# Block sums of the second MLP weights: VectorE additions replaced by accumulating transfers

## Chip, cores and metric

The kernel runs on one core of a Trainium2 chip. The metric is the device time of one execution in microseconds (us). It was 1401.65 us, the median of three runs (1401.09 to 1402.0).

## What is computed

Two layers of an encoder trunk over 512 tokens of 1024 features, all in float32. Each layer is a token mixer (a gated DeltaNet in layer 0, a gated linear attention in layer 1) followed by an MLP; both are added to a scaled residual and normalised. The change lies in the MLP, which runs once in each layer:

```python
def _sq_relu_mlp(h, w1, w2):          # h 512x1024, w1 1024x4096, w2 4096x1024
    a = jax.nn.relu(jnp.matmul(h, w1))
    return jnp.matmul(a * a, w2)

x = _layernorm(DEEPNORM_ALPHA * x + _sq_relu_mlp(x, mlp_w1[i], mlp_w2[i]), ln2_g[i], ln2_b[i])
```

## The kernel before

Every float32 matrix product runs as three TensorE products of split operands (`mm3`, L109 to L111): each operand is written as a high part (a ScalarE cast, L90) plus a low part (a VectorE subtraction, L91). `split` makes the pair. The names are `wh`/`wl` for the first weights and those of the mixers, `w2h`/`w2l` for the second MLP weights, `ah`/`al` for activations, `xth`/`xtl` for the transposed input of a stage. Weights reach SBUF by transfers that SyncE issues (L45); `wst` and `w2r` are the tiles in which they land.

`mlp` cuts the 4096 hidden features into G = 4 groups of 1024, that is eight blocks of 128 features each. A call of `feature` makes one such block: 24 matmuls of 512 columns into a bank `pj`, then ReLU and square on ScalarE into `h`. For the first three groups the second matrix product (512 tokens x 1024 hidden times 1024 hidden x 1024 outputs) is done by `second` with seven products of half size instead of eight, after Strassen and Winograd. The activations are four quarters `a11` to `a22`, the weights four blocks `b11`, `b12`, `b21`, `b22`, which the code names `blocks[i, j, q]` with (i, j) = (0, 0), (0, 1), (1, 0), (1, 1), and with q = 0, 1 for the two halves of a block's rows. One half is a tile `w2r` of 128 partitions x 1024 float32, 512 KB. Each product is 24 matmuls into two banks out of X, Y or Z. `nxt` puts one `feature` of the next group behind each product, so TensorE alternates: product, feature, product, feature. A group has 7 products and 8 features.

The products need sums of weight blocks. Before the change VectorE makes them: `sums` (L295, L296, L298) replaces b11 by b11 + b12 and b12 by b12 + b22, and writes b11 + b12 + b22 into two more tiles, blocks (2, 2); L359 then adds that to b21. Product 5 uses b11 + b12, product 7 uses b12 + b22, product 6 uses the sum of three, product 4 the sum of all four. The order is 1, 2, 6, 5, 7, 3, 4.

The rings limit how far things run ahead: three pairs `w2h`/`w2l`, two pairs `ah`/`al`, ten raw tiles `w2r`, three of `wst` and of `wh`/`wl`. The order within each engine is fixed when the program is built; an engine executes its queue in that order, and an instruction that waits holds back all that stand behind it on its engine. In the MLP of layer 0 GpSimd (POOL) also builds eight masks for layer 1 (`sel_masks`: tiles `tmp`, made by a memset and two selects at L463, L465 and L467), which VectorE turns into `mu1` to `mu128`. The last group goes through `last`, which the change does not touch. `load_ln` (L173) fetches the parameters of a normalisation by transfers that POOL issues.

Of the kernel before, what the change touches and what calls it, by code (L numbers as in the profile page):

```python
# [13 lines left out]
ALU = mybir.AluOpType  # L14
# [3 lines left out]
P = 128  # L18
# [232 lines left out]
def mlp(c, w1, w2, g, b, out=None, extra=None):  # L251
# [3 lines left out]

    tc, nc = c.tc, c.nc
    V, A, T = nc.vector, nc.scalar, nc.tensor
    G = 4  # L260
# [3 lines left out]
    with c.banks(pj=2, X=2, Y=2, Z=2), tc.tile_pool(name="mlp", bufs=2) as pool:  # L264
        par = c.load_ln(g, b, lambda i: pool.tile([P, 512], F32, name=f"ln{i}", bufs=1))
        touched = set()
        blocks = {}
        parts = {}
        RING = {"ah": ("ah", "al", 2), "w2": ("w2h", "w2l", 3), "raw": ("w2r", "w2r", 10)}

        def ring(name):
            return (pool, *RING[name])

        def act(ps, h):
            A.activation(h, ps, AF.Relu)  # L275
            A.activation(h, h, AF.Square)

        def raw():
            return pool.tile([P, 2, 512], F32, name="w2r", tag="w2r", bufs=10)

        def load(gi, i, j):
            for q in range(2):
                blocks[i, j, q] = t = raw()
                r = (gi * GF + i * HF + 2 * q) * P
                c.dma(t, w2[r:r + 2 * P, 512 * j:512 * j + 512].rearrange("(k p) n -> p k n", p=P))

        def split(i):

            i_, j_ = {1: (0, 0), 2: (1, 0), 3: (1, 1), 4: (1, 0), 5: (0, 0), 6: (2, 2), 7: (0, 1)}[i]
            parts[i] = [c.split(blocks[i_, j_, q], [P, 2, 512], pool=ring("w2")) for q in range(2)]  # L290

        def sums(q):

            b11, b12, b22 = (blocks[k + (q,)] for k in ((0, 0), (0, 1), (1, 1)))
            V.tensor_tensor(b11, b11, b12, ALU.add)  # L295
            V.tensor_tensor(b12, b12, b22, ALU.add)  # L296
            blocks[2, 2, q] = t = raw()
            V.tensor_tensor(t, b11, b22, ALU.add)  # L298

        def new_h():  # L300
            return [pool.tile([P, HF, S], F32, name="h", tag="h", bufs=3) for _ in range(2)]

        def feature(gi, f, h):
            act(c.proj_cm(w1, (gi * GF + f) * P, "pj"), h[f // HF][:, f % HF, :])

        def pair(src, where="ah"):
            return c.split(src, [P, HF, HT], pool=ring(where))

        def add(t, hf, ps, op=ALU.add):
            xs = c.xh(t)[hf]  # L310
            if (t, hf) not in touched:
                touched.add((t, hf))
                V.scalar_tensor_tensor(xs, xs, ALPHA, ps, ALU.mult, op)
            else:
                V.tensor_tensor(xs, xs, ps, op)

        def quarters(h):
            return [h[j][:, :, HT * i:HT * i + HT] for i in range(2) for j in range(2)]

        def second(gi, h, a, nxt):  # L320

            a11, a12, a21, a22 = quarters(h)

            def banks(tag):
                return [c.bank([P, 512], F32, name="p" + tag, tag=tag) for _ in range(2)]

            def product(bk, a, i, new):

                if i not in parts:
                    split(i)  # L330
                ws = parts.pop(i)
                for q, (wh, wl) in enumerate(ws):
                    for j in range(2):
                        sl = slice(j * P, (j + 1) * P)
                        for k in (2 * q, 2 * q + 1):
                            c.mm3(bk[j], a[0][:, k, sl], a[1][:, k, sl], wh[:, k % 2, :], wl[:, k % 2, :],
                                  new and k == 0, k == HF - 1, skip_group_check=True)

            X, Y = banks("X"), banks("Y")
            product(X, a, 1, True)  # L340
            load(gi, 1, 0)
            for j in range(2):
                add(j, 0, X[j])
            nxt()
            Z = banks("Z")
            product(Z, pair(a12), 2, True)
            s1 = pool.tile([P, HF, HT], F32, name="s1", tag="s1", bufs=1)
            V.tensor_tensor(s1, a22, a21, ALU.subtract)
            V.tensor_tensor(a21, a11, a21, ALU.subtract)
            V.scalar_tensor_tensor(a11, s1, -1.0, a11, ALU.mult, ALU.subtract)  # L350
            for q in range(2):
                sums(q)
            for j in range(2):
                add(j, 0, Z[j])
            nxt()
            product(X, pair(a11), 6, False)
            V.scalar_tensor_tensor(a12, a12, -1.0, a11, ALU.mult, ALU.subtract)
            for q in range(2):
                V.tensor_tensor(blocks[1, 0, q], blocks[2, 2, q], blocks[1, 0, q], ALU.add)  # L359
            for j in range(2):  # L360
                add(j, 1, X[j], ALU.subtract)
            nxt()
            product(Y, pair(s1), 5, True)
            if gi + 2 < G:
                load(gi + 1, 0, 0)
            for j in range(2):
                add(2 + j, 1, Y[j], ALU.subtract)
            nxt()
            product(X, pair(a21), 7, False)
            if gi + 2 < G:  # L370
                load(gi + 1, 0, 1)
            for j in range(2):
                add(2 + j, 0, X[j])
                add(2 + j, 1, X[j], ALU.subtract)
            nxt()
            product(Y, pair(a12), 3, False)
            if gi + 2 < G:
                load(gi + 1, 1, 1)
            for j in range(2):
                add(j, 1, Y[j], ALU.subtract)  # L380
            nxt()
            W = banks("Z")
            product(W, pair(a22), 4, True)
            for j in range(2):
                add(2 + j, 0, W[j])
            nxt()
            nxt()

        def last(gi, h):

            a = {}
            for i in range(2):
                for j in range(2):
                    a[i, j] = pair(h[j][:, :, HT * i:HT * i + HT], "raw" if i else "ah")
            ws = [c.wrows(w2, (gi * GF + 2 * (i % 4)) * P, i // 4 * 512, pool=ring("w2") if i < 3 else None if i < 6 else ring("raw"))
                  for i in range(8)]
            if out is None:
                c.new_x()
            for t in range(NT):
                sl = slice(t % 2 * P, t % 2 * P + P)  # L400
                for hf in range(2):
                    ps = c.bank([P, 512], F32, name="pl", tag="XYZ"[(2 * t + hf) % 3])
                    for k in range(GF):
                        wh, wl = ws[4 * hf + k // 2]
                        ah, al = a[t // 2, k // HF]
                        c.mm3(ps, ah[:, k % HF, sl], al[:, k % HF, sl], wh[:, k % 2, :], wl[:, k % 2, :], k == 0, k == GF - 1)
                    add(t, hf, ps)
                c.layernorm(c.xh(t), c.xh(t), par, last=out is not None)
                if out is None:
                    c.xpose(t, c.xt[t], ("pj",))  # L410
                else:
                    nc.sync.dma_start(out[t * P:(t + 1) * P, :], c.xt[t])

        h = new_h()
        specs = [(c.wcols(w1, f * P, pool=ring("ah") if f == 3 else None), "pj", ("pj", "pj", "X", "X")[f]) for f in range(4)]
        for f, ps in enumerate(c.proj_halves(specs)):
            act(ps, h[0][:, f, :])
        for f in range(4, GF):
            feature(0, f, h)
            if f == 5:  # L420
                load(0, 0, 0)
                load(0, 0, 1)
            if f == 6:
                load(0, 1, 1)
                split(1)
                a = pair(quarters(h)[0])
        if extra:
            extra(lambda: pool.tile([P, P], F32, name="tmp", tag="tmp", bufs=2))
        for gi in range(G - 1):
            more = gi + 2 < G  # L430
            nh = new_h()
            todo = iter(range(GF))

            def nxt():
                f = next(todo)
                feature(gi + 1, f, nh)
                if f == 6 and more:
                    split(1)
                    nxt.a = pair(quarters(nh)[0])

            second(gi, h, a, nxt)
            h, a = nh, nxt.a if more else None
        last(G - 1, h)
# [960 lines left out]
```

## Time and profile before

| | us |
|---|---|
| median of three runs | 1401.65 |
| the profiled execution | 1401.75 |
| its span | 1400.0 |
| TensorE (PE) busy | 1365.9 |
| VectorE (DVE) busy | 983.8 |
| ScalarE (ACT) busy | 689.5 |
| GpSimd (POOL) busy | 80.6 |

The difference between the execution and its span lies outside of what the trace shows. PE is busy nearly all of the span, at a granted clock of 0.998. The MLP of layer 0 takes the stretch from about 450 to 775 us, that of layer 1 the one from about 1060 to the end. A stretch in which PE is never idle can only become shorter if its matmuls become fewer or follow each other more closely; work on other engines shows in the time where PE has to wait for it.

### The profile page before, as it was taken

Reading aid. Unit: us, or ns where it says so; the run is one execution under the profiler, and the core shown is the slowest. Engines: PE = TensorE matmul, PEld = TensorE weight load, DVE = VectorE, ACT = ScalarE, POOL = GpSimd, SP = SyncE. Lnnn points to the kernel's source line nnn. Section 1 sums busy time; section 2 is a strip of 40 time slices with the busy share of each in tenths; the row PEclk is TensorE's granted clock in tenths of the full one; section 3 lists DMA queues with packets and bytes.
Section 4 is the critical chain, followed back from the end, with each engine's and each line's share of the span. In section 5 each row is a group of like instructions: output and inputs, shape, how many; then the busy total and the mean of one; then the engine's idle time right before and its main releaser. Section 6 shows DMA issues by size and latency. Waiting matters only on the chain.

```text
span 1400.0 us, 20133 instructions
## 1 busy us (share of the span) xinstructions
PE 1365.9 (98%) x7933; PEld 1117.6 (80%) x7933; DVE 983.8 (70%) x1589; ACT 689.5 (49%) x1320; POOL 80.6 (6%) x120
## 2 busy tenths in 40 slices
PE   7999999999999999999999999999999999999997
PEld 6777777777777888888887888888878888888886
DVE  5787787778668676758656577876766657777655
ACT  3776657665633554444543354654434444445430
POOL 5000000000003200000000100000001000000000
PEclk9999999999999999999999999999999999999999
DMA  6212111211133733332131222221216342422121
GB/s 171 76 48 60 46 46 46 61 46 46 47 106 86 230 121 94 102 122 59 45 100 40 87 87 71 61 61 61 89 48 207 107 153 61 136 75 60 46 83 52
DMA packets 146117, 117.05 MB, mean 84 GB/s; under 512 B 7631, under 2 KB 122439, under 8 KB 146023
## 3 DMA queue, kind: packets, MB, share of 16 engines
q1 hardware_dynamic: 144112, 111.49, 26.5%
q0 software_dynamic: 1344, 4.20, 1.1%
q8 instruction: 62, 1.02, 0.3%
q14 instruction: 32, 0.26, 0.1%
q10 hardware_dynamic: 567, 0.08, 0.0%
HBM read 113.66 MB, written 2.10 MB: 83 GB/s over the span
## 4 chain that ended last, share of the span: by engine, by line
PE 61%; issue 27%; ACT 6%; DVE 3%; POOL 2%; DMA 1%; DVEq 0%; POOLq 0%; SPq 0%; ACTq 0%
PE pj L110 4%; PE pj L111 4%; PE pj L109 4%; PE pjv L109 3%; PE pjv L111 3%; PE pjv L110 3%; PE scp L678 2%; PE op L1335 2%; PE pjq L110 1%; PE pjq L111 1%; PE pjq L109 1%; PE op L766 1%; PE lv L1210 1%; PE pX L109 1%; PE pX L111 1%
## 5 line engine op out<-in xcount | busy, mean ns | idle before, releaser
L91 DVE TENSOR_TENSOR wl<-wst,wh 128x1024 fp32r<-128x1024 f32 x137 | 168.5, 1231 | 165.5 <-ACT wh L90 164.8
L90 ACT CAST wh<-wst 128x1024 fp32r<-128x1024 f32 x137 | 143.9, 1051 | 267.8 <-PE pj L110 164.4
L109 PE MATMUL pj<-xth,wh 128*128 128x512 f32 (+1 forms) x544 | 201.7, 372 | 0.7 <-ACT xth L149 0.7
L110 PE MATMUL pj<-xtl,wh 128*128 128x512 f32 (+1 forms) x544 | 201.6, 371 | 0.4 <-DVE xtl L150 0.4
L111 PE MATMUL pj<-xth,wl 128*128 128x512 f32 (+1 forms) x544 | 201.7, 371 | 0.0
L91 DVE TENSOR_TENSOR w2l<-w2r,w2h 128x1024 fp32r<-128x1024 f32 x84 | 102.6, 1222 | 49.4 <-ACT w2h L90 48.9
L110 PEld LDWEIGHTS pj<-xtl,wh 128*128 128x128 f32 x544 | 102.5, 188 | 18.7 <-DVE xtl L150 0.9
L109 PEld LDWEIGHTS pj<-xth,wh 128*128 128x128 f32 x544 | 102.3, 188 | 18.3 <-ACT xth L149 0.9
L111 PEld LDWEIGHTS pj<-xth,wl 128*128 128x128 f32 x544 | 102.4, 188 | 18.1 <-DVE wl L91 0.3
L90 ACT CAST w2h<-w2r 128x1024 fp32r<-128x1024 f32 x84 | 88.3, 1051 | 55.3 <-DMA w2r<-in_mlp_w 17.5
L90 ACT CAST ah<-h 128x1024 fp32r<-128x1024 f32 x40 | 42.2, 1054 | 56.2 <-DVE h L350 21.8
L110 PE MATMUL pX<-w2l,ah 128*128 128x512 f32 x144 | 56.1, 390 | 0.0
L109 PE MATMUL pX<-w2h,ah 128*128 128x512 f32 x144 | 56.1, 390 | 0.0
L111 PE MATMUL pX<-w2h,al 128*128 128x512 f32 x144 | 56.1, 390 | 0.0
L109 PE MATMUL pjv<-wh,xth 128*128 128x512 f32 x128 | 54.9, 429 | 0.0
L91 DVE TENSOR_TENSOR al<-h,ah 128x1024 fp32r<-128x1024 f32 x40 | 48.9, 1222 | 2.8 <-ACT ah L90 1.5
L160 ACT ACTIVATE rsy<-rsv 128x1 f32<-128x1 f32 (+1 forms) x28 | 5.6, 200 | 90.8 <-DVE rsv L159 90.8
L111 PE MATMUL pjv<-wh,xtl 128*128 128x512 f32 x128 | 50.2, 392 | 0.0
L110 PE MATMUL pjv<-wl,xth 128*128 128x512 f32 x128 | 49.9, 390 | 0.0
L109 PE MATMUL pjk<-xth,wh 128*128 128x512 f32 (+1 forms) x112 | 42.1, 376 | 0.5 <-ACT wh L90 0.5
L110 PE MATMUL pjk<-xtl,wh 128*128 128x512 f32 (+1 forms) x112 | 41.6, 371 | 0.0
L275 ACT ACTIVATE h<-pj 128x512 f32<-128x512 f32 x64 | 37.8, 591 | 7.4 <-PE pj L111 7.4
(442 smaller groups left out, 3444.8 us busy)
## 6 DMA issues: line engine op xcount, KB each, us to landing
wst<-in_mlp_w SPq DMA_DIRECT2D x80, 512.0 KB, 4.0
w2r<-in_mlp_w SPq DMA_DIRECT2D x48, 512.0 KB, 3.6
wst<-in_a_w_in SPq DMA_DIRECT2D x32, 512.0 KB, 4.0
wst<-in_b_w_in SPq DMA_DIRECT2D x32, 256.0 KB, 3.0
wst<-in_a_w_out SPq DMA_DIRECT2D x8, 512.0 KB, 3.8
wst<-in_b_w_in SPq DMA_DIRECT2D x8, 512.0 KB, 3.8
wst<-in_b_w_out SPq DMA_DIRECT2D x8, 512.0 KB, 3.6
xt<-in_x SPq DMA_DIRECT2D x4, 512.0 KB, 7.3
```

What stands on the lines that cost most here:

```text
L90: nc.scalar.copy(hi, src)
L91: nc.vector.tensor_tensor(lo, src, hi.bitcast(F32), ALU.subtract)
L109: mm(ps, ah, bh, start=start, stop=False, **kw)
L110: mm(ps, ah, bl, start=False, stop=False, **kw)
L111: mm(ps, al, bh, start=False, stop=stop, **kw)
L160: nc.scalar.activation(y, v, AF.Ln)
L275: A.activation(h, ps, AF.Relu)
L678: T.matmul(ps[:, n, :], kh[:, sl], qh[:, sl], start=True, stop=True)
L766: T.matmul(ops, l, r, start=i == 0, stop=i == len(mm) - 1)
L1210: T.matmul(ps[:, u, :, :], lhs[:, u, :], cols(rhs, u, s, i), start=True, stop=True)
L1335: T.matmul(op[:, n, :], l, r, start=i == 0, stop=i == len(mm) - 1)
```

## The change

The 48 VectorE additions (eight in each of the three groups, in two layers) are removed. In their place `plus` issues, from the POOL queue, a transfer from one SBUF tile to another that adds its source to its destination in place. There are eight of 512 KB each in a group: after the split for product 1, b11 += b12 and b12 += b22; after the split for product 5, b11 += b22 (now the sum of three) and b21 += b11. The extra tiles (2, 2) are gone, so a group uses eight of the ten raw tiles. Since b11 + b12 is overwritten by the sum of three, product 5 now stands before product 6: 1, 2, 5, 6, 7, 3, 4. The loads of the next group's blocks, and of b21, stand a little earlier in the code.

```diff
-            i_, j_ = {1: (0, 0), 2: (1, 0), 3: (1, 1), 4: (1, 0), 5: (0, 0), 6: (2, 2), 7: (0, 1)}[i]
+            i_, j_ = {1: (0, 0), 2: (1, 0), 3: (1, 1), 4: (1, 0), 5: (0, 0), 6: (0, 0), 7: (0, 1)}[i]
             parts[i] = [c.split(blocks[i_, j_, q], [P, 2, 512], pool=ring("w2")) for q in range(2)]
 
-        def sums(q):
-
-            b11, b12, b22 = (blocks[k + (q,)] for k in ((0, 0), (0, 1), (1, 1)))
-            V.tensor_tensor(b11, b11, b12, ALU.add)
-            V.tensor_tensor(b12, b12, b22, ALU.add)
-            blocks[2, 2, q] = t = raw()
-            V.tensor_tensor(t, b11, b22, ALU.add)
+            if i == 1:
+                plus((0, 0), (0, 1))
+                plus((0, 1), (1, 1))
+            elif i == 5:
+                plus((0, 0), (1, 1))
+                plus((1, 0), (0, 0))
+
+        def plus(a, b):
+
+            for q in range(2):
+                nc.gpsimd.dma_start(blocks[a + (q,)], blocks[b + (q,)], accum_op=ALU.add)
...
-            for q in range(2):
-                sums(q)
             for j in range(2):
                 add(j, 0, Z[j])
             nxt()
+            product(Y, pair(s1), 5, True)
+            for j in range(2):
+                add(2 + j, 1, Y[j], ALU.subtract)
+            nxt()
             product(X, pair(a11), 6, False)
+            fetch(0, 0)
             V.scalar_tensor_tensor(a12, a12, -1.0, a11, ALU.mult, ALU.subtract)
-            for q in range(2):
-                V.tensor_tensor(blocks[1, 0, q], blocks[2, 2, q], blocks[1, 0, q], ALU.add)
```

**On VectorE**, in group 1 of layer 0, the new order is shown from the subtraction that makes `s1` to the split for product 6. `w2r_6598` and `w2r_6600` are the two halves of b11, `w2r_6918` and `w2r_6920` those of b21; `s1` is the activation operand of product 5.

```order
L91 TENSOR_TENSOR al_7059<-s1_7019,ah_7058 128x1024
L360 SCALAR_TENSOR_TENSOR h_6341<-s1_7019,h_6341 128x4x256
L91 TENSOR_TENSOR w2l_7063<-w2r_6598,w2h_7062 128x1024
L370 SCALAR_TENSOR_TENSOR h_6342<-h_6342,h_6341 128x4x256
L91 TENSOR_TENSOR wl_7179<-wst_7176,wh_7178 128x1024
L91 TENSOR_TENSOR w2l_7067<-w2r_6600,w2h_7066 128x1024
L320 TENSOR_TENSOR xt0_5650<-xt0_5650,pZ_6981 128x512
L320 TENSOR_TENSOR xt1_5651<-xt1_5651,pZ_6982 128x512
L91 TENSOR_TENSOR al_7134<-h_6341,ah_7133 128x1024
L91 TENSOR_TENSOR w2l_7138<-w2r_6598,w2h_7137 128x1024
L91 TENSOR_TENSOR wl_7256<-wst_7253,wh_7255 128x1024
L91 TENSOR_TENSOR w2l_7142<-w2r_6600,w2h_7141 128x1024
```

The first half of product 5's split takes the third place here, where the addition of L359 stood right after L350 before, and the split for product 6 now reads the tiles of b11 again.

**On POOL**, the same group. `w2r_6674` and `w2r_6676` are b12, `w2r_6751` and `w2r_6753` are b22. Before, POOL has nothing to do in this stretch.

```order
L303 DMA w2r_6598<-w2r_6674 128x1024
L303 DMA w2r_6674<-w2r_6751 128x1024
L303 DMA w2r_6600<-w2r_6676 128x1024
L303 DMA w2r_6676<-w2r_6753 128x1024
L303 DMA w2r_6598<-w2r_6751 128x1024
L303 DMA w2r_6918<-w2r_6598 128x1024
L303 DMA w2r_6600<-w2r_6753 128x1024
L303 DMA w2r_6920<-w2r_6600 128x1024
```

The eight transfers stand alone; the halves alternate, so the seventh (the second half of b11 += b22) stands behind the sixth, which reads what the fifth wrote.

**On POOL**, the start of the MLP of layer 0, after the change: `gb`, `gcol` and `ngb` are constants for layer 1, `tmp` the mask tiles, `w2r_6197` and `w2r_6199` are b11 of group 0, `w2r_6201` and `w2r_6203` b12, `w2r_6238` and `w2r_6240` b22.

```order
L503 TENSOR_SCALAR ngb_6337<-gb_6335 128x8
L303 DMA w2r_6197<-w2r_6201 128x1024
L473 MEMSET tmp_6307 128x128
L303 DMA w2r_6199<-w2r_6203 128x1024
L475 AFFINE_SELECT tmp_6307<-tmp_6307 128x128
L477 AFFINE_SELECT tmp_6307<-tmp_6307 128x128
L303 DMA w2r_6201<-w2r_6238 128x1024
L473 MEMSET tmp_6313 128x128
L303 DMA w2r_6203<-w2r_6240 128x1024
L475 AFFINE_SELECT tmp_6313<-tmp_6313 128x128
L477 AFFINE_SELECT tmp_6313<-tmp_6313 128x128
```

Four transfers stand between the mask instructions, which before followed each other directly.

**On VectorE**, the same place after the change. The `wl` tiles here belong to the features 4, 5 and 6 of group 0, in this order.

```order
L91 TENSOR_TENSOR wl_6134<-wst_6131,wh_6133 128x1024
L485 TENSOR_TENSOR mu8_6311<-tmp_6307,tmp_6301 128x128
L91 TENSOR_TENSOR wl_6167<-wst_6164,wh_6166 128x1024
L485 TENSOR_TENSOR mu16_6317<-tmp_6313,tmp_6307 128x128
L91 TENSOR_TENSOR w2l_6417<-w2r_6347,w2h_6416 128x1024
L485 TENSOR_TENSOR mu32_6323<-tmp_6319,tmp_6313 128x128
L91 TENSOR_TENSOR wl_6208<-wst_6205,wh_6207 128x1024
```

Before, seven of the eight additions of group 0 stood between and behind these masks, and the `wl` of feature 4 came after `mu16` and not before `mu8`.

## Rows read from the trace of the kernel before

**Rows 1.** The page, busy time, share of the span and instructions by engine.

```profile
PE 1365.9 (98%) x7933; PEld 1117.6 (80%) x7933; DVE 983.8 (70%) x1589; ACT 689.5 (49%) x1320; POOL 80.6 (6%) x120
```

**Rows 2.** Busy time by stretch: span, engines (instructions), granted clock, DMA share, GB/s.

```profile
480.00:735.00 255.00, 255.00 (x1121) 210.06 (x1120) 169.95 (x169) 120.14 (x141) 0.00 (x0) 1.00 0.31 95
1060.00:1380.00 320.00, 319.46 (x1484) 267.51 (x1485) 208.43 (x220) 144.41 (x174) 2.37 (x5) 1.00 0.32 102
```

**Rows 3.** Waits of PE, 390 to 800 us: total us, times, longest.

```profile
PE tp L146 <- POOL xt L194: 2.5, 4, 0.7
...
PE pj L110 <- DVE xtl L150: 0.2, 1, 0.2
```

**Rows 4.** Timeline of PE: start us, length us, engine, line, operation.

```profile
479.04 0.39 PE L111 MATMUL pj<-xth,wl 128*128 128x512 f32 x1
...
489.48 0.39 PE L109 MATMUL pX<-w2h,ah 128*128 128x512 f32 x1
...
571.54 0.39 PE L109 MATMUL pX<-w2h,ah 128*128 128x512 f32 x1
...
604.38 0.39 PE L109 MATMUL pY<-w2h,ah 128*128 128x512 f32 x1
...
607.35 0.39 PE L110 MATMUL pY<-w2l,ah 128*128 128x512 f32 x1
```

**Rows 5.** Groups by line, removed additions, first and last: busy us, mean ns, idle before.

```profile
L295 DVE TENSOR_TENSOR w2r<-w2r 128x1024 f32<-128x1024 f32 x12 | 14.7, 1223 | 1.8 <-DMA w2r<-in_mlp_w 1.5
...
L298 DVE TENSOR_TENSOR w2r<-w2r 128x1024 f32<-128x1024 f32 x12 | 14.6, 1219 | 0.0
```

**Rows 6.** Timeline of DVE in group 1 of layer 0.

```profile
581.76 1.22 DVE L359 TENSOR_TENSOR w2r<-w2r 128x1024 f32<-128x1024 f32 x1
...
586.52 1.22 DVE L91 TENSOR_TENSOR w2l<-w2r,w2h 128x1024 fp32r<-128x1024 f32 x1
...
597.47 1.22 DVE L91 TENSOR_TENSOR w2l<-w2r,w2h 128x1024 fp32r<-128x1024 f32 x1 [1.76 <-ACT w2h L90]
```

**Rows 7.** Timeline of ACT in the same group.

```profile
596.38 1.05 ACT L90 CAST w2h<-w2r 128x1024 fp32r<-128x1024 f32 x1 [0.77 <-PE pX L111]
```

**Rows 8.** Transfers of the whole run: issues, KB each, median us from issue to landing.

```profile
w2r<-in_mlp_w SPq DMA_DIRECT2D x48, 512.0 KB, 3.6
...
wst<-in_b_w_in SPq DMA_DIRECT2D x32, 256.0 KB, 3.0
...
wst<-in_b_w_in SPq DMA_DIRECT2D x8, 512.0 KB, 3.8
...
z<-in_x SPq DMA_DIRECT2D x8, 256.0 KB, 3.8
...
lnp<-in_ln_g POOLq DMA_DIRECT2D x2, 256.0 KB, 4.8
```

**Rows 9.** Line 173, POOL's issue of a transfer: ns min/median/max.

```profile
L173 POOL DMA_DIRECT2D ln<-in_ln_g x6: 538/548/626, 449.9 to 1061.1; - x6
```

**Rows 10.** Timeline of POOL at the start of layer 0's MLP.

```profile
463.07 0.25 POOL L493 TENSOR_SCALAR ngb<-gb 128x8 f32<-128x8 f32 x1 [4.21 <-DMA gb<-in_b_gate_b]
463.29 0.20 POOL L463 MEMSET tmp<- 128x128 f32 x1
...
465.10 1.00 POOL L465 TENSOR_SCALAR_AFFINE_SELECT tmp<-tmp 128x128 f32<-128x128 f32 x1
466.16 0.34 POOL L467 TENSOR_SCALAR_AFFINE_SELECT tmp<-tmp 128x128 f32<-128x128 f32 x1
```

**Rows 11.** Transfers issued from 448 to 455 us.

```profile
w2r<-in_mlp_w SPq DMA_DIRECT2D x6, 512.0 KB, 10.0
```

**Rows 12.** Busy time by stretch at that start, columns as in rows 2.

```profile
460.00:464.00 4.00, 4.00 (x36) 4.00 (x35) 1.40 (x2) 3.27 (x6) 0.82 (x3) 1.00 1.16 272
464.00:468.00 4.00, 4.00 (x34) 3.76 (x33) 2.86 (x4) 0.18 (x1) 2.99 (x6) 1.00 0.85 315
468.00:472.00 4.00, 4.00 (x18) 3.30 (x18) 2.90 (x5) 2.93 (x5) 2.10 (x6) 1.00 0.68 210
```

More of the change, by code (lines that the diff above doesn't have):

```diff
@@ L325, in banks, with product @@
                 return [c.bank([P, 512], F32, name="p" + tag, tag=tag) for _ in range(2)]
-            def product(bk, a, i, new):
+            def product(bk, a, i, new, by_tile=False):
                 if i not in parts:
@@ L331, in product, with fetch @@
                 ws = parts.pop(i)
[L332 to L337, printed above, removed]
+                order = [(q, j) for j in range(2) for q in range(2)] if by_tile else [(q, j) for q in range(2) for j in range(2)]
+                for q, j in order:
+                    wh, wl = ws[q]
+                    sl = slice(j * P, (j + 1) * P)
+                    for k in (2 * q, 2 * q + 1):
+                        c.mm3(bk[j], a[0][:, k, sl], a[1][:, k, sl], wh[:, k % 2, :], wl[:, k % 2, :],
+                              new and k == 0, k == HF - 1, skip_group_check=True)
+            def fetch(i, j):
+                if gi + 2 < G:
+                    load(gi + 1, i, j)
             X, Y = banks("X"), banks("Y")
+            load(gi, 1, 0)
             product(X, a, 1, True)
-            load(gi, 1, 0)
             for j in range(2):
@@ L362, in second, with seventh, third @@
             nxt()
[L363 to L367, printed above, removed]
-            nxt()
[L369 to L380, printed above, removed]
+            def seventh():
+                product(X, pair(a21), 7, False)
+                fetch(0, 1)
+                for j in range(2):
+                    add(2 + j, 1, X[j], ALU.subtract)
+                    add(2 + j, 0, X[j])
+            def third():
+                product(Y, pair(a12), 3, False)
+                fetch(1, 1)
+                for j in range(2):
+                    add(j, 1, Y[j], ALU.subtract)
+            seventh()
+            nxt()
+            third()
             nxt()
```

## Prediction

> **What bounds the kernel now.** I read the busy times first, then the same by stretch, then what TensorE waits for, then the timelines of single engines. PE is busy 98% of the span, VectorE 70% [rows 1]. An average could hide a stage in which VectorE is the limit, so the stretch counts: from 480 to 735 us, where all three groups of layer 0's second products lie, PE is busy 255.00 of 255.00 us; in layer 1, from 1060 to 1380, 319.46 of 320 [rows 2]. From 390 to 800 us PE's longest list entry is 2.5 us of waiting for POOL at the transposes ahead of and behind the MLP; inside it only 0.2 us stand, at the first features [rows 3]. The first matmul of a group's first product stands at 489.48 and, one group later, at 571.54 [rows 4]: 82.06 us for 15 steps (7 products, 8 features) of 24 matmuls, 5.47 us a step. So PE sets the time of the groups, VectorE waits for it, and the question is not how much VectorE saves but whether the sums still come in time.
>
> Do the additions slow PE while they run beside it? From 571.54 to 604.38, the first matmul of the group's fourth product [rows 4], lie 6 steps: 5.473 us each. The other 9 steps take 82.06 - 32.84 = 49.22 us, 5.469 each, and most of the additions lie in those. No.
>
> **What is removed.** 48 additions of 1.22 us, 12 for each of four lines [rows 5], 58.6 us of VectorE. None is on PE's path: worth 0 us there. At the start of layer 0 the low part for feature 4 comes earlier on VectorE; that is under the 0.2 us of rows 3, and I count 0.
>
> **What is added: the price X of one accumulating transfer**, from its issue to its landing. The trace has none, so it is bounded. From SyncE a plain 512 KB weight transfer takes 3.6 us [rows 8]; that is the low end. For the value I take: 3.8 us for 512 KB of another tensor; 1.0 for issuing from POOL (4.8 against 3.8 for 256 KB); and, as the destination must be read too, another 512 KB at what the step from 256 to 512 KB cost, 2 x (3.8 - 3.0) = 1.6 [rows 8]. X = 6.4 us. For the high end I put the plain transfers that were issued into full queues, 10.0 us [rows 11], in place of 3.8: 12.6 us. I take 6.4 for the groups, as their stretches have a DMA share of 0.31 and 0.32 [rows 2] where those had about 1.
>
> The Trainium skill ("DMA: Bandwidth & Descriptors", section Anatomy of one DMA) gives a transfer from POOL as 2.0 us plus its bytes over 436 GB/s. By that 512 KB would be an estimated 3.2 us, and 4.4 with the destination counted as well; no row shows an accumulating one. The sum would be the same, and both slower rivals below would lose most of their chance.
>
> **Steady state: is the sum of three ready for product 6?** Take group 1 of layer 0, with the steps where they are now. Product 5 is third, product 6 fourth, so 6 starts at 604.38 [rows 4]. On VectorE the first half of product 5's low part takes the place of the addition at 581.76, so b11's first half is free at 583.0; the second half, which waits for a ring slot, keeps the place at 586.52, so it is free at 587.7 [rows 6]. POOL's order decides the rest. The first half of b11 += b22 is issued at 583.0. Next in the queue stands b21 += b11, which waits until that has landed, at 583.0 + X; only behind its issue, 0.55 us [rows 9], comes the second half of b11 += b22. It lands at 583.0 + 2X + 0.55. The second half is needed when PE reaches its second matmul, at 607.35 [rows 4]; high and low part take 1.1 us (596.38 to 597.47) plus 1.22 [rows 6, 7], so at 605.0 it must be there. That holds for X up to (605.0 - 583.55) / 2 = 10.7 us. With 6.4 it lands at 596.4, when ACT would turn to it anyway (596.38) [rows 7]: 0 us, with 8.6 us to spare. The first half may take 19 us. What waits behind on ACT and VectorE (the next feature's split, the next activation) is used by PE after product 6 starts, or later.
>
> The other sums have more room. b11 += b12 has about two steps of group g - 1 and two products of its own group; b21 += b11 is used last, by product 4. Product 7 now follows product 6 in the same banks, so its first matmul waits until VectorE has read them out; a feature of 5.47 us lies between, and the two reads of 0.68 us are next in VectorE's queue. 0 us. SyncE gets loads that wait for a landed transfer (b12 of the next group into the tiles of b11), issued about seven steps after: 0 us.
>
> The Trainium skill ("SBUF — State Buffer", section Who interferes with whom) speaks against the change in one point: VectorE shares its second SBUF ports with POOL, so making a transfer on POOL can be held up for a whole VectorE instruction, though not by two-input ones, which take the read side alone. POOL's issues here last 538 to 626 ns [rows 9]; the trace shows no hold-up. If each did cost one 1.22 us instruction, the chain of two would still fit.
>
> **The start of layer 0's MLP.** Here POOL is not free. The first transfer stands behind `ngb`, which ends at 463.3 [rows 10]; the second behind a memset (0.20) and the issue (0.55), at 464.1. Then the third waits for the first, the fourth for the second, and the masks stand behind them; VectorE waits for the masks, and behind these stands feature 6's low part. With X' for the landing there: the fourth is issued at 464.1 + X'; issue, two selects (1.00 and 0.34) [rows 10] give `mu16` at 466.0 + X'; the next mask (0.20 + 1.00 + 0.34 and some 0.2 of gaps) `mu32` at 467.7 + X'; then 0.3 for it and 1.22 for the low part: 469.2 + X'. PE needs it at 479.04 [rows 4], so X' may be 9.8 us. The engines are full until 464 (1.16), then at 0.85 and 0.68 [rows 12]. Between 6.4 and 12.6 I take 8.5, nearer the low end since the share falls: 0 us, 1.3 us to spare. Layer 1 builds no masks.
>
> **The sum.** 1401.75 (span 1400.0) - 0 + 0 = 1401.75 for the profiled execution, which is 0.1 above the median; I say 1401.6.
>
> **Rivals.** (a) *Stall at the start of layer 0*: X' over 9.8 us. Price X' - 9.8 once; at 12.6 that is 2.8 us: 1404.5. For it: full engines, 10.0 us for plain transfers [rows 11]. Against: the load is past its peak. Most of this case stays within 0.2% (2.8 us, about what a measurement can tell from no change). (b) *Slower in every group*: an accumulating transfer is much dearer than two plain readings, X over 10.7. PE then stands before the second half of product 6, 2 x (X - 10.7) us in each of 6 groups. At 12.6 that is 22.8 us, with (a) 1427; at 11.2 it is 6 us, 1409 with (a). For it: the trace has no such transfer, and POOL's order makes two landings follow each other. Against: it needs 1.7 times my X. (c) *Faster*: PE gets back the waits of rows 3 in layer 0, 2.5 + 0.2 us: 1399.0. Against: they lie at transposes that no addition stands ahead of.
>
> **How the numbers follow.** No change 0.78, of which about 0.10 is a stall of (a) under 2.8 us; (a) over that 0.06; (b) 0.13; (c) 0.03. So faster 0.03, same 0.78, slower 0.19. The likeliest case alone spans 1400.4 to 1404.4. The low end goes to 1399.5; the high end to 1412, which takes in (a) to its bound and (b) up to X = 11.3; beyond lie about 0.1.
>
> **What would show it.** Right: VectorE's busy time down by 58 us, PE still at 100% from 480 to 735, a group still 82.06 us, landings near 6.4 us, POOL's waits between the fifth and the eighth transfer of a group. Wrong: PE waiting for `w2h` or `w2l` at product 6; the low part of feature 6 late near 479 us; landings over 10.7 us; or a group shorter than 82.06 us, which would say that PE was not at its own pace.

## The result, and the profile after

| | before | after |
|---|---|---|
| median, us | 1401.74 (20 runs, 1401.09 to 1403.88) | 1404.07 (20 runs, 1403.21 to 1408.98) |
| ratio, 95% interval | | 1.0019 [1.0013, 1.0026] |
| profiled execution, us | 1401.75 | 1403.39 |
| its span, us | 1400.0 | 1401.7 |

The change makes the kernel slower, by 2.3 us. The forecast was no change, 1401.6. The time lies inside the range, but the interval excludes no change, and the likeliest case did not have the loss.

**The groups run as forecast.** The page of the changed kernel, busy times (us, share of the span, instructions), answers to [rows 1]; below it the queue that POOL's transfers use (packets, MB, share of 16 engines):

```profile
PE 1366.0 (97%) x7933; PEld 1116.8 (80%) x7933; DVE 929.5 (66%) x1541; ACT 689.5 (49%) x1320; POOL 121.3 (9%) x168
...
q0 software_dynamic: 8256, 29.37, 10.8%
```

VectorE has lost 54.3 us, POOL has gained 40.7, PE's work is the same. The stretches of layer 0's groups in the changed kernel, with the columns of [rows 2], and the first matmul of group 0's and of group 1's first product, as in [rows 4]:

```profile
480.00:735.00 255.00, 254.37 (x1117) 209.14 (x1116) 152.24 (x154) 121.86 (x142) 17.41 (x21) 1.00 0.54 138
490.81:572.88 82.07, 82.07 (x361) 67.58 (x360) 48.57 (x49) 38.82 (x46) 6.88 (x8) 1.00 0.62 153
```

```profile
490.81 0.39 PE L109 MATMUL pX<-w2h,ah 128*128 128x512 f32 x1
...
572.88 0.39 PE L109 MATMUL pX<-w2h,ah 128*128 128x512 f32 x1
```

A group takes 82.07 us, as before (82.06), and PE is busy for all of it. The time went elsewhere: the first `pX` of group 0 stands at 490.81, and at 489.48 before. The reader should measure the start of each MLP from one matmul to another that both kernels have. The first matmul of the MLP's first features behind PE's wait for its transposed input is, in the kernel before and then in the changed one:

```profile
453.04 0.36 PE L111 MATMUL pj<-xth,al 128*128 128x256 f32 x1
```

```profile
452.40 0.37 PE L111 MATMUL pj<-xth,al 128*128 128x256 f32 x1
```

From there to the first `pX` it is 36.44 us before and 38.41 after: 1.97 us lost in layer 0. The same stretch of layer 1 takes 41.47 us before (1060.68 to 1102.15) and 41.89 after (1061.89 to 1103.78): 0.42 lost. Together that is 2.39, about the whole difference. The way to that first matmul, which the change does not touch, took 452.40 to 454.67 us in the runs of this case, so it is left out here.

**Where PE waits.** The list of PE's waits in the changed kernel, 390 to 800 us (total us, times, longest), has two lines that [rows 3] has not, and the timeline of PE shows them at the features 6 and 7:

```profile
PE pj L109 <- ACT h L276: 0.9, 2, 0.6
...
PE pj L111 <- DVE wl L91: 0.4, 1, 0.4
```

```profile
478.21 0.50 PE L109 MATMUL pj<-xth,wh 128*128 128x512 f32 x1 [0.25 <-ACT h L276]
...
479.34 0.50 PE L111 MATMUL pj<-xth,wl 128*128 128x512 f32 x1 [0.39 <-DVE wl L91]
...
485.23 0.50 PE L109 MATMUL pj<-xth,wh 128*128 128x512 f32 x1 [0.63 <-ACT h L276]
```

The third matmul of feature 6, at 479.04 in [rows 4], stands at 479.34 here, although this execution reached the MLP 0.64 us earlier: it is 0.94 late, counted from the first matmul, and that this low part comes late is one of the signs by which the prediction said that it would be wrong. Feature 7 adds the rest. There are two chains to follow. The first is the one of the prediction, on POOL (timeline of the changed kernel; start, length, operation, what ended the idle time before):

```profile
462.90 0.96 POOL L303 DMA_DIRECT2D w2r<-w2r  x1 [0.28 <-issue]
...
463.68 1.24 POOL L303 DMA_DIRECT2D w2r<-w2r  x1
...
471.31 0.86 POOL L303 DMA_DIRECT2D w2r<-w2r  x1 [5.50 <-DMA w2r<-w2r]
...
474.20 0.85 POOL L303 DMA_DIRECT2D w2r<-w2r  x1 [1.81 <-DMA w2r<-w2r]
474.76 0.65 POOL L475 TENSOR_SCALAR_AFFINE_SELECT tmp<-tmp 128x128 f32<-128x128 f32 x1
```

The third transfer waits until 471.31 for the first, the fourth until 474.20 for the second. In the chain of waits of this stretch (start, us, what) the second landing is one piece:

```profile
463.68 10.24 DMA w2r<-w2r
```

Behind it come the selects, `mu16`, `mu32` and feature 6's low part, on VectorE:

```profile
475.85 0.29 DVE L485 TENSOR_TENSOR mu<-tmp 128x128 uint8<-128x128 f32 x1 [8.58 <-POOL tmp L477]
...
478.06 1.22 DVE L91 TENSOR_TENSOR wl<-wst,wh 128x1024 fp32r<-128x1024 f32 x1
```

It ends at 479.28, and PE's wait at 479.34 ends with it. The second chain is on ScalarE, and the prediction has nothing of it:

```profile
471.48 1.05 ACT L90 CAST w2h<-w2r 128x1024 fp32r<-128x1024 f32 x1 [7.97 <-DMA w2r<-in_mlp_w]
...
483.63 1.05 ACT L90 CAST wh<-wst 128x1024 fp32r<-128x1024 f32 x1 [4.81 <-DMA wst<-in_mlp_w]
484.58 0.59 ACT L276 ACTIVATE h<-pj 128x512 f32<-128x512 f32 x1
```

The cast at 483.63 is for the first feature of group 1 and waits for its load. The ReLU behind it, at 484.58, frees the bank that feature 7 writes, and PE starts feature 7 at 485.23, when that ReLU is done. The load was issued at 467.61; the list of transfers from 466 to 468.5 us in the changed kernel, and from 466 to 469 in the kernel before, where the same load was issued at 467.99 (KB, us from issue to landing):

```profile
wst<-in_mlp_w SPq DMA_DIRECT2D x1, 512.0 KB, 15.9
```

```profile
wst<-in_mlp_w SPq DMA_DIRECT2D x1, 512.0 KB, 4.3
```

Both the late landing and the late load fall into a stretch in which the DMA engines are full. The stretches behind [rows 12], in the changed kernel (the last two columns are the DMA share and GB/s):

```profile
464.00:468.00 4.00, 4.00 (x32) 3.83 (x31) 1.43 (x2) 0.00 (x0) 1.74 (x4) 1.00 1.11 355
468.00:472.00 4.00, 4.00 (x19) 3.30 (x19) 0.00 (x0) 0.53 (x1) 0.69 (x2) 1.00 1.07 216
472.00:476.00 4.00, 4.00 (x20) 3.30 (x19) 0.15 (x1) 3.94 (x7) 1.94 (x5) 1.00 1.08 314
```

Where the share fell to 0.85 and 0.68 before [rows 12], it now stays above 1. A share above 1 does not by itself make a load come too late, as e8 shows below.

So three theories stood at the start. **A**: the transfers' traffic makes loads late. **B**: VectorE waits for masks that stand behind the transfers' waits on POOL. **C**: the loads of the next group, which stand earlier in the code and find two free tiles in the ring, fill the engines.

### The profile page after: what moved, and what is told of

It is laid out like the page before. It is cut to its first block, busy times and chain, and to the rows that moved or that the text cites. A ratio compares the mean times of both kernels' runs of the same rounds, so it can differ in the third digit from the quotient of the medians.

```text
span 1401.7 us, 20232 instructions
## 1 busy us (share of the span) xinstructions
PE 1366.0 (97%) x7933; PEld 1116.8 (80%) x7933; DVE 929.5 (66%) x1541; ACT 689.5 (49%) x1320; POOL 121.3 (9%) x168
## 4 chain that ended last, share of the span: by engine, by line
PE 59%; issue 23%; DMA 6%; ACT 6%; POOL 3%; DVE 2%; SPq 1%; DVEq 0%; POOLq 0%; ACTq 0%
DMA w2r<-w2r 4%; PE pj L109 3%; PE pj L111 3%; PE pj L110 3%; PE pjv L109 3%; PE pjv L111 3%; PE pjv L110 3%; PE scp L688 2%; DMA w2r<-in_mlp_w 2%; PE op L1345 2%; PE pjq L110 1%; PE pjq L111 1%; PE pjq L109 1%; PE op L776 1%; PE lv L1220 1%
## 5 line engine op out<-in xcount | busy, mean ns | idle before, releaser
L303 POOL DMA_DIRECT2D w2r<-w2r x48 | 41.5, 902 | 398.2 <-DVE w2l L91 230.1
L1168 POOL TENSOR_TENSOR atl<-on,ath 128x512 f16<-128x512 f32 x16 | 20.9, 1306 | 323.4 <-ACT ath L1167 171.5
```

The lines of the kernel that those rows point to most:

```text
L303: nc.gpsimd.dma_start(blocks[a + (q,)], blocks[b + (q,)], accum_op=ALU.add)
L1168: G.tensor_tensor(atl[:, us, :], at, ath[:, us, :], ALU.subtract)
```

## The experiments

All are edits of the changed kernel. "Layer 0" and "layer 1" are the two stretches above (before: 36.44 and 41.47 us), each from one profiled execution. "Cast" is the time from the same first matmul of layer 0 to the cast for group 1's first feature (before: 25.52). Each ratio is to runs of the kernel before on the same chip.

| run | us | ratio, 95% interval | layer 0 | layer 1 | cast |
|---|---|---|---|---|---|
| changed kernel | 1404.07 | 1.0019 [1.0013, 1.0026] | 38.41 | 41.89 | 31.23 |
| e1 all sums on VectorE | 1401.22 | 0.9997 [0.9988, 1.0006] | 36.30 | 41.44 | |
| e2 group 0 on VectorE | 1401.22 | 0.9997 [0.9988, 1.0006] | 36.28 | 41.46 | |
| e3 transfers in group 0 only | 1403.72 | 1.0017 [1.0008, 1.0026] | 38.04 | 41.89 | 30.73 |
| e4 masks early | 1401.75 | 1.0001 [0.9992, 1.0009] | 36.37 | 42.04 | 28.35 |
| e5 group 0's first four late | 1401.23 | 0.9996 [0.9987, 1.0004] | 36.30 | 41.45 | 25.39 |
| e6 ring of eight | 1404.68 | 1.0020 [1.0011, 1.0029] | 38.25 | 42.03 | 31.07 |
| e7 one sum three times | 1431.03 | 1.0205 [1.0189, 1.0220] | 40.75 | | 29.20 |
| e8 plain copies | 1401.38 | 0.9996 [0.9987, 1.0005] | 36.28 | 41.45 | 26.34 |
| e11 masks early, same traffic | 1404.02 | 1.0021 [1.0012, 1.0030] | 38.27 | 41.83 | 31.09 |
| e12 plain copies, mask late | 1403.17 | 1.0013 [1.0004, 1.0022] | 37.77 | 41.45 | 26.28 |

### Which transfers cost: e1, e2, e3

```diff
-                nc.gpsimd.dma_start(blocks[a + (q,)], blocks[b + (q,)], accum_op=ALU.add)
+                V.tensor_tensor(blocks[a + (q,)], blocks[a + (q,)], blocks[b + (q,)], ALU.add)
```

In e1 this holds everywhere; the new order of products and loads stays.

> The changed kernel with its sums made on VectorE, in place, at the same places; order of products, ring and places of the loads as changed. Theory A (the transfers compete with the weight loads at the start of each MLP) and theory B (the masks stand behind the transfers on POOL): both 1401.7 us, as the kernel before. Theory C (the loads of the next group's b11, which now run early, do the competing, not the transfers): 1403.5 or more, as the changed kernel.

In e2 it holds in group 0 of both layers, in e3 in all groups but that.

> The sums of group 0 on VectorE in both layers, those of groups 1 and 2 by accumulating transfers. If the groups in their steady state cost nothing, as the trace of the changed kernel shows (a group takes 82.07 us before and after), 1401.7 us under A and B; if the groups do cost something, more. Under C about 1404.

> The reverse: accumulating transfers in group 0 alone, groups 1 and 2 on VectorE. The whole loss stays: 1404.1 us under A, B and C.

e1 gives 1401.22: the order and the earlier loads cost nothing, and C by itself falls. e2, with 32 of the 48 transfers, gives the same, so a transfer in a group that is under way costs nothing. e3, with the other 16, has 1403.72 and nearly the whole loss (1404.1 was expected). The start of the two MLPs is the place.

### The masks moved ahead: e4

```diff
+        if extra:
+            extra(lambda: pool.tile([P, P], F32, name="tmp", tag="tmp", bufs=7))
         for f in range(4, GF):
...
-        if extra:
-            extra(lambda: pool.tile([P, P], F32, name="tmp", tag="tmp", bufs=2))
```

> The changed kernel with seven mask tiles instead of two, and the masks written ahead of the loads of the weight blocks, so that all stand ahead of the first transfer on POOL; the transfers start when they did. Theory B: most of layer 0's 2.0 us is gone, 1402.1 us (0.4 us of layer 1 stay). Theory A: PE still waits at features 6 and 7, for ScalarE behind a late weight load, 1403.5 us or more.

Layer 0 lost nothing, so I took B for shown. That was too early. POOL's timeline of this run shows that the edit also moved the transfers:

```profile
461.92 1.00 POOL L303 DMA_DIRECT2D w2r<-w2r  x1
467.07 0.25 POOL L503 TENSOR_SCALAR ngb<-gb 128x8 f32<-128x8 f32 x1 [4.15 <-DMA gb<-in_b_gate_b]
467.60 0.92 POOL L303 DMA_DIRECT2D w2r<-w2r  x1 [0.27 <-issue]
```

The second transfer stands behind `ngb`, which waits for `gb`: it starts at 467.60 and not at 463.68, and the load of group 1's first feature lands 13.0 us after its issue and not 15.9. Two things were changed at once.

### Almost the same traffic without the masks' wait: e11

e11 keeps the edit of e4. In addition `gb` and `gcol` are now fetched ahead of the masks, so that `ngb` doesn't hold the second transfer.

```diff
-        self.masks = sel_masks(c, pool, tmp)
         self.gb = pool.tile([P, 2, B_H], F32, name="gb", bufs=1)
...
+        self.masks = sel_masks(c, pool, tmp)
         self.ngb = pool.tile([P, 2, B_H], F32, name="ngb", bufs=1)
```

> In the run with the masks early the second transfer was issued 3.9 us later than in the changed kernel, since it stood behind ngb, which waited for gb; so that run changed the traffic too. Here gb and gcol are fetched ahead of the masks, all masks are made ahead of the first transfer, and the first two transfers follow each other as in the changed kernel (within 1 us of each other). Theory B (VectorE waits for masks that stand behind the transfers' waits on POOL) expects layer 0, from its first pj to its first pX, at 36.4 us and a total of 1401.9. Theory A' (the transfers' traffic makes the load of group 1's first feature land 16 us after its issue instead of 4; on ScalarE the cast that waits for it holds back the ReLU that frees the bank of feature 7) expects that cast at about 483.5 us again and feature 7 to start late, now without a late feature 6: layer 0 at 38.0 to 38.2 us, total 1403.5.

1404.02, as slow as the changed kernel and half a us over what A expected, though no mask stands behind a transfer any more: VectorE has made the last one by 464.94. PE's and ScalarE's timelines of e11:

```profile
481.27 0.50 PE L109 MATMUL pj<-xth,wh 128*128 128x512 f32 x1 [1.43 <-ACT h L276]
```

```profile
474.53 1.05 ACT L90 CAST w2h<-w2r 128x1024 fp32r<-128x1024 f32 x1 [9.14 <-DMA w2r<-in_mlp_w]
...
480.62 0.59 ACT L276 ACTIVATE h<-pj 128x512 f32<-128x512 f32 x1
...
485.76 1.05 ACT L90 CAST wh<-wst 128x1024 fp32r<-128x1024 f32 x1 [3.88 <-DMA wst<-in_mlp_w]
```

The casts that wait for loads hold back the ReLUs, at feature 6 already. So A alone gives nearly the whole loss, 1.83 of 1.97 us in layer 0. The traffic is not quite that of the changed kernel: the first two transfers start 1.73 us apart instead of 0.78, and one load of SyncE is issued 4.2 us later, counted from the first matmul (at 467.24; 460.75 in the changed kernel). In e4, where the masks are early too, that load is 3.1 us later, and nothing is lost.

### The masks' wait without the traffic: e8 and e12

e8 leaves `accum_op` out: the same 48 transfers as plain copies, so the block sums are not made. e12 adds to e8 a late mask, with feature 6's low part fixed behind it:

```diff
-            nc.gpsimd.affine_select(out=f, in_=f, compare_op=ALU.is_ge, fill=0.0, base=w - 1,
-                                    pattern=[[w, P // w], [0, w]], channel_multiplier=-1)
+            for _ in range(13 if w == 16 else 1):
+                nc.gpsimd.affine_select(out=f, in_=f, compare_op=ALU.is_ge, fill=0.0, base=w - 1,
+                                        pattern=[[w, P // w], [0, w]], channel_multiplier=-1)
...
```

> The same 48 transfers at the same places on POOL, but as plain copies: the destination is overwritten, the block sums are not made. It prices the accumulation. If an accumulating transfer is dearer because its destination is read too, the median landing falls from 5.6 to about 4.5 us, and the transfer engines' time per MB from about 86 to about 53 us. At the start of layer 0 the landings of the first two then fall from 8.4 and 10 us to 6.5 and 8.5, below the 9.0 that leaves feature 6's low part in time, and the time is about 1402. If the full engines decide and not the kind of transfer, the landings there stay above 8 and 9.5 us and the time at 1403.5 to 1404.

> The opposite case: the transfers are plain copies, which cost no time in their own run and let that load land at 479 us (the block sums are not made), but the mask for width 16 is made late: its second select is repeated 12 times (the mask stays the same), about 12 x 0.41 = 5 us, and the low part of feature 6 is fixed behind it on VectorE. Theory B expects feature 6's third matmul to wait about 1 us and nothing behind it to give that back: layer 0 at 37.3 to 37.6 us instead of 36.3, total 1402.2 to 1402.7. Theory A' expects the lateness at feature 6 too, as any late operand costs, but says that it is not what sets the time of the changed kernel. Only if the 1 us is hidden (layer 0 at 36.4, total 1401.4) do the masks count for nothing. If both runs lose, the two causes overlap in the changed kernel, and the longer one, 1.8 us at feature 7, sets the time.

e8 loses nothing. Its line of the transfers (ns min/median/max of POOL's issue; issue to landing) and its queue, against the same two of the changed kernel:

```profile
L303 POOL DMA_DIRECT2D w2r<-w2r x48: 528/528/621, 463.4 to 1287.3; - x48
...
DMA to landing us min/median/max: 2.8/3.9/7.8
```

```profile
L303 POOL DMA_DIRECT2D w2r<-w2r x48: 847/856/1239, 462.9 to 1291.6; - x48
...
DMA to landing us min/median/max: 4.5/5.6/11.5
```

```profile
q0 software_dynamic: 8256, 29.37, 5.7%
```

In the kernel before this queue took 1.1% for the transfers that no version changes. So the 48 transfers take 4.6% of the engines as copies and 9.7% as accumulations, 2.1 times as much. That is the direct price of the accumulation, and it decides at the start. The engines are as full in e8 as in the changed kernel, but they move more, as the stretch of 468 to 472 us shows (1.06 and 370 GB/s; 1.07 and 216 in the changed kernel):

```profile
468.00:472.00 4.00, 4.00 (x19) 3.30 (x19) 0.00 (x0) 1.35 (x2) 0.77 (x2) 1.00 1.06 370
```

The load of group 1's first feature is late here too, 12.0 us from issue to landing, but not too late: the cast stands at 26.34 us and in the changed kernel at 31.23. No transfer takes longer than 7.8 us to land, under the 9.8 that the prediction worked out, and the masks are in time as well.

e12 shows B alone, on PE and VectorE:

```profile
480.71 0.50 PE L111 MATMUL pj<-xth,wl 128*128 128x512 f32 x1 [1.14 <-DVE wl L91]
```

```profile
479.23 0.29 DVE L492 TENSOR_TENSOR mu<-tmp 128x128 uint8<-128x128 f32 x1 [5.54 <-POOL tmp L484]
479.44 1.22 DVE L91 TENSOR_TENSOR wl<-wst,wh 128x1024 fp32r<-128x1024 f32 x1
```

Layer 0 takes 37.77: 1.3 us lost, 0.2 more than the high end of what was expected, since the selects took 5.24 us. The total, 1403.17, is half a us above its expectation. So a late mask is a loss too, with nothing behind it that gives it back. Both causes are real, and they overlap.

The column "cast" puts them together. Feature 7 is due 36.44 - 5.47 = 30.97 us after the first matmul; the ReLU must have ended by then, and it ends 1.54 us after that cast starts (483.63 to 485.17), so the cast may start at 29.4. In the changed kernel it starts 1.8 later, in e11 1.7, in e6 1.6; their losses in layer 0 are 1.97, 1.83 and 1.81. In e4, e5, e7, e8 and e12 it is in time, and only e12, with its mask, and e7 (below) lose, both at the low part of feature 6. In the changed kernel the masks' 0.94 us at feature 6 lie inside the 1.97. In e3 it is the other way round: the cast is 1.3 us late, and the wait for the low part, behind the masks, is longer and covers that; the loss is 1.60:

```profile
480.16 0.50 PE L111 MATMUL pj<-xth,wl 128*128 128x512 f32 x1 [1.41 <-DVE wl L91]
```

### Fewer loads, or later transfers: e6 and e5

e6 lowers the ring of `w2r` from ten to eight, so that the next group's b11 can't be loaded at the start. e5 holds group 0's first four transfers behind feature 6:

```diff
...
+                if group[0] == 0:
+                    gate = pool.tile([P, 1], F32, name="gate", tag="gate", bufs=1)
+                    after = tc.issue_after(nc.gpsimd.tensor_copy(gate, h[1][:, 2, 0:1]).ins)
...
```

> The ring of raw tiles has 8 instead of 10, so the next group's two halves of b11 can't be loaded beside the start. The order on POOL and VectorE is that of the changed kernel. If the landing at the start is as long as it is (8.4 and about 10 us) because of those extra loads, mu16 comes 1.5 us or more earlier and the time is about 1402. If it is long because of the first features' and first blocks' own loads and of the transfers themselves, the time stays at 1403.7 to 1404.1, and layer 0 from first pj to first pX at 38.0 to 38.4 us. A late load of b11 in the steady groups would show as a stall at a product 1.

> The first four transfers of group 0, in both layers, are held back on POOL behind a copy of one column of feature 6's output (a tile gate), so that the masks are made ahead of them and no transfer runs beside the first features. Theory B (the masks stand behind the transfers' waits on POOL) and theory A (the transfers' traffic makes the first features' weights late) both expect the 2.0 us at the start of layer 0 gone: layer 0 from its first pj to its first pX 36.4 us instead of 38.4. They differ in layer 1, which builds no masks: A expects its 0.4 us gone too (41.5 instead of 41.9), total 1401.5; if the 0.4 has another cause it stays, total 1401.9. If holding them back makes product 5 late, its price shows there and not at the features.

e6 gains nothing (1404.68; the load lands after 16.1 us): those extra loads are not what fills the engines. e5 removes the loss of both layers, 36.30 and 41.45, total 1401.23. Layer 1 builds no masks, so its 0.42 us is A's: in the changed kernel ScalarE's cast of `w2r` there waits 7.94 us for its load, in e5 2.91, as before (2.79). On ScalarE all that follows comes later, up to the ReLU that ends at 1092.72; PE starts feature 6 then, 0.53 us behind the matmul at 1092.24, where one follows another after 0.23:

```profile
1092.77 0.50 PE L109 MATMUL pj<-xth,wh 128*128 128x512 f32 x1
```

That this cast is the path in layer 1 is read from the trace, not tested apart.

### The slack in the groups: e7

```diff
...
-                plus((0, 0), (1, 1))
+                for _ in range(3 if group[0] > 0 else 1):
+                    plus((0, 0), (1, 1))
```

> In groups 1 and 2 of both layers b11 += b22 is issued three times instead of once, so the sum of three is computed with b22 three times; nothing else changes. The chain ahead of product 6's second half then holds more landings one after the other. By the prediction's steady-state step (the second half is needed about 22 us after the fifth transfer's issue, each landing 5.6 us, each issue 0.86) a chain of four to five landings overruns by about 6 us in each of four groups: 24 us over the changed kernel, 15 to 35, 1419 to 1439, with PE waiting at product 6 (pX after product 5's feature). If the slack is larger than the prediction says, the time stays near 1404. If PE waits already in the changed kernel without being seen, each extra landing costs its full 5.6 us or more: 45 us and above.

1431.03, 27 us over the changed kernel. PE at feature 6 of group 0 and in product 6 of group 1, and the granted clock (the column ahead of the DMA share) in the stretches behind these two waits:

```profile
481.28 0.50 PE L111 MATMUL pj<-xth,wl 128*128 128x512 f32 x1 [2.53 <-DVE wl L91]
...
614.85 0.51 PE L109 MATMUL pX<-w2h,ah 128*128 128x512 f32 x1 [3.56 <-ACT w2h L90]
616.11 0.79 PE L110 MATMUL pX<-w2l,ah 128*128 128x512 f32 x1 [0.76 <-DVE w2l L91]
```

```profile
483.00:486.00 3.00, 3.00 (x9) 2.33 (x8) 3.00 (x3) 1.11 (x2) 0.00 (x0) 0.50 1.01 323
...
615.00:618.00 3.00, 2.25 (x6) 1.54 (x7) 3.00 (x3) 3.00 (x4) 0.00 (x0) 0.62 0.92 178
```

Product 6 takes 11.74 us (608.39 to 620.13) instead of 5.47, 6.27 lost: 4.32 of waits, and most of the rest in matmuls that follow each other every 0.43 us instead of 0.23. The other three groups wait up to 1 us less, so the four come to somewhat under 25. The start of layer 0, which the edit does not touch, takes 2.3 us more than in the changed kernel's profile: `ngb` ran 1.0 us later there, counted from the first matmul, the transfers and masks behind it came later with it, and PE waited 2.53 us for the low part of feature 6. So the chain that the prediction followed bounds a group once it is too long, and its slack is about of the size that it gave.

## Why the prediction was wrong, and where it was right

- **PE sets the pace of the groups; the additions are worth 0.** Right: 82.07 us a group, and e1, with all sums on VectorE, and e2, with two thirds of them as transfers, are both at 1401.22.
- **The price X.** Taken 6.4 us, measured 5.6 in the median, 4.5 to 11.5, inside the bounds 3.6 and 12.6. POOL's issue was taken from a plain transfer, 0.55 [rows 9]; it is 0.86. By the Trainium skill ("DMA: Bandwidth & Descriptors", section Anatomy of one DMA) the prediction estimated 3.2 us, and 4.4 with the destination counted. The trace does not agree: measured are 3.9 for the plain copy and 5.6 for the accumulation, about a quarter more in both cases.
- **The chain of the groups.** Right in its order, and in its sum. In group 1 of the changed kernel, on POOL:

```profile
584.61 0.86 POOL L303 DMA_DIRECT2D w2r<-w2r  x1 [15.61 <-DVE w2l L91]
589.90 1.74 POOL L303 DMA_DIRECT2D w2r<-w2r  x2 [4.43 <-DMA w2r<-w2r]
597.66 0.86 POOL L303 DMA_DIRECT2D w2r<-w2r  x1 [6.02 <-DMA w2r<-w2r]
```

The second half of b11 += b22 has landed at 597.66. It was needed at 605.0, which is 606.3 here (this execution is 1.34 later at that place): 8.7 us to spare, and the prediction said 8.6. That this fits to 0.1 us is partly luck: of the two landings in the chain the first was shorter than the 6.4 us taken for both (5.0), the second and the issues were longer. So rival (b) did not come, and e7 shows that its mechanism is there.

- **The start of layer 0: the step that failed.** It was put at 0 us with 1.3 us to spare, and 1.97 us were lost. The chain was right, link by link, and its threshold was 9.8 us. The term that was mis-sized is X' = 8.5 with "the share falls" as its reason. The first transfer landed after 8.1, but the step that counts goes through the second, which took 10.24. The share fell in [rows 12] without the new transfers; with 2 MB of them it stays above 1. A stretch's load before a change is no measure for what that change puts into it. So feature 6 came 0.94 us late instead of 1.3 early: 0.4 from the landing, 0.2 because the second transfer is issued 11.28 us behind the first matmul and not 11.06, and 0.3 on the way from the landing to the matmul.
- **What the step left out weighed more.** The prediction asked when the new transfers land, and not what they do to the loads that others wait for; of SyncE's queue it looked at the groups alone, and said 0 us. The load of group 1's first feature went from 4.3 to 15.9 us. ScalarE stands waiting for it in order, with a ReLU behind it that PE needs. That path alone gives nearly the whole loss (e11). The Trainium skill ("DMA: Bandwidth & Descriptors", section SWDGE vs HWDGE vs iDMA, under Issuing engines are not separate DMA queues) says that transfers issued by different engines run on the same 16 DMA engines and interleave. The trace agrees, 15.9 against 4.3 us, and this rule would have turned the question to the loads.
- **Layer 1.** "Builds no masks" was true and no reason for 0: 0.42 us went there, where a ReLU behind a cast that waits for its load came late again.
- **The rivals.** (a) named the place, and its price, X' - 9.8 at 10.24, is 0.4 us; measured are 1.97 us there, and 0.42 in layer 1, of which (a) has nothing. Its mechanism is one of two that are there, and the smaller. (c) did not come: PE's longest entry is the same 2.5 us at the transposes.

No version beats the kernel before: the intervals of e1, e2 and e5 all hold 1, as a stretch in which PE is never idle leaves nothing to gain. What stays open is why spreading the first two transfers (e4) brings the load in 2.9 us sooner with the engines as full as in the changed kernel (share 1.06 to 1.15). The traces narrow it down to SyncE's issue of this load, which takes 3.27 us in the changed kernel, 2.63 in e11 and 0.41 in e4; from the end of the issue it lands after 12.6 or 12.7 us in all three. What draws the issue out is not shown.

## What to carry to other kernels

Taking work from an engine that isn't the bound gives nothing, and the transfers that replace it are paid where the DMA engines are already full: price what a new transfer does to every load in flight there, and not only its own landing. Follow each late load to the engine that waits for it in order, and read what stands behind that wait; here a ReLU behind a cast, not the cast, stopped PE. And when an experiment removes a loss, look at what else it moved before calling the cause shown: e4 pointed at the masks, e11 showed that they need not be there at all.

## What the runs showed of the hardware

- An accumulating transfer between SBUF tiles of 512 KB lands in 5.6 us against 3.9 for the copy, takes 0.86 us of POOL for its issue against 0.53, and 2.1 times the engines' time.
- SyncE's issue of a load can grow while the engines are full: 6.35 us for one of `w2r` in the changed kernel (share 1.17 and 1.11), and 0.58 for one of the same kind in the kernel before (0.68). Full engines are not enough for it: the issue just ahead took 0.37. The changed kernel, then the kernel before:

```profile
460.75 0.37 SPq L45 DMA_DIRECT2D wst<-in_mlp_w  x1
461.16 6.35 SPq L45 DMA_DIRECT2D w2r<-in_mlp_w  x1
```

```profile
468.40 0.58 SPq L45 DMA_DIRECT2D w2r<-in_mlp_w  x1
```

- A wait of PE can cost more than its length. In e7, after waits of 2.53 and 3.56 us, the granted clock was 0.50 and 0.62 (at 0.50 it is the lower level, 1.2 GHz) and matmuls took nearly twice as long for 3 to 4 us. After e11's wait of 1.43 us it stayed at 1.00.
